# Quarter sums of the FFN's activations: formed by the producer and kept in DRAM, with the down stage's weight splits on VectorE

## The chip, the cores and the metric

The kernel runs on one core of a Trainium2 chip. The metric is the device time of one execution in microseconds (us); the time before is the median of three runs, 3012.46 us.

## What is computed

The program is a hybrid two-layer block followed by a second block. The change lies in the last stage of the second block, its feed-forward network (FFN), and in nothing else:

```python
h = rmsnorm(x, g_ffn_pre)                                   # 1024 tokens x 1024
f = (silu(h @ w_gate) * (h @ w_up)) @ w_down                # 2816 columns in between (22 rows of 128)
x = x + rmsnorm(f, g_ffn_post)
```

Below, y is the product `silu(h @ w_gate) * (h @ w_up)`, kept transposed: row j of it is a tile of 128 of the 2816 columns by 1024 tokens.

## The kernel before

**Exact products from rounded halves.** A matmul here takes operands that are split into a rounded part and a rest: `split` (line 368) lets ScalarE write the rounded copy (hi) and a second engine the difference (lo = source - hi, one subtraction with both inputs in SBUF). Each product then is three matmuls: lo by hi, hi by lo, hi by hi. Every operand of 128x512 so costs one ScalarE instruction and one subtraction, and the kernel chooses per operand which engine subtracts.

**Gate and up stage** (`ffn`, from line 2329). The 22 rows of y are made in pairs of rows. The first pair (rows 0 and 1) is made directly, over two halves of the tokens, while `combos` (line 2481) forms sums of the input's quarters on VectorE and GpSimd. The ten other pairs use a seven-product scheme: for each pair seven steps for gate (`a` = 0) and seven for up (`a` = 1), each step 12 matmuls. `pair_prep` (line 2533) prepares a step's weights two steps ahead, with their subtractions on GpSimd. VectorE adds the products' PSUM results and multiplies gate by up into the tiles `F`. When a pair is done, `store` (line 2344) sends both rows to the DRAM rows `self.F` (22 tiles of 128x1024, line 1733).

**Down stage** (`quarters`, line 1444). The product with w_down also uses seven products of quarters. The 22 rows of y are split into an upper and a lower half, and row k is taken with row 11 + k; with the two halves of the tokens this gives four quarters y11, y12, y21, y22. The seven products are done in four passes over k = 0 to 10: passes a, b and c hold two products each, pass d one. A unit is one product at one k: 12 matmuls of 128x512 in passes a to c. Pass d has 22 half units of six matmuls, the first eleven for token tiles 4 and 5, the last eleven for tiles 6 and 7, which keep the operands of the first. `quarters_units` (line 1384) prepares two units ahead:

- pass a uses y11 and y12 and plain weights;
- pass b uses the sums y21 + y22 - y11 and y11 - y21, formed in place from the rows held in SBUF (tiles `yr`), two adds on VectorE and two on GpSimd (one into `s3`), and two adds of weights on VectorE;
- pass c uses y21 + y22 and y22, and three adds of weights on VectorE;
- pass d uses y12 minus the first sum of pass b, and plain weights.

Each operand of y is split into a tile `yhl` with the subtraction on VectorE; each operand of the weights into `whi` and `wlo` (pass d: `whl`) by `w_pair` (line 1438), whose subtraction is on GpSimd. `whi` and `wlo` have three buffers each, so that the split for unit n + 3 waits until TensorE is through with unit n. All loads are issued by SyncE's queue in a fixed order. The rows of y are loaded once, in pass a (`y_row`, line 1320), and stay until pass c or d: up to 22 of the 40 tiles of 128x1024 that all stages share (`S`). Ahead of the first pass, two steps are loaded.

After pass c four token tiles (0 to 3) are complete, and `chain` (line 2454) normalizes and stores them; tiles 4 to 7 follow in pass d. A chain has ScalarE squares, a multiply by the norm's weights, a power on GpSimd and two fused adds with the residual `rx` on VectorE.

**What sets the order.** The order on TensorE is that of the program. On the other engines it comes from priorities: a planner (`Mixer`) books each instruction at a modelled time, and each queue is sorted by that. It has one table of busy times per engine, so that a change of engine moves instructions in the whole stage. Each queue then runs strictly in this order.

Of the kernel before, what the change touches and what calls it, by code (L numbers as in the profile page):

```python
# [13 lines left out]
ALU = mybir.AluOpType  # L14
AX = mybir.AxisListType

NX = 1024
# [465 lines left out]
class Layers(Base):  # L483
# [835 lines left out]

    def y_row(self, yT, order):  # L1320

        def row(k):
            r = self.S("yr")
            self.nc.sync.dma_start(out=r, in_=yT[order[k]][:, 0:NX])
            return r

        return row

    def y_prefetch(self, g, yT, order, n):
# [32 lines left out]

    def quarters_begin(self, kn, w, row):

        self.q = (kn // 2, row, {})
        self.q_ld = self.quarters_loads(w)
        self.q_ahead = deque(next(self.q_ld) for _ in range(2))

    def quarters_loads(self, w):
        m, row, rows = self.q  # L1370
        dma = self.nc.sync.dma_start
        for p in "abcd":
            for k in range(m):
                if p == "a":
                    rows[k], rows[m + k] = row(k), row(m + k)
                q = self.QW[p]
                ts = [self.S("ws") for _ in range((len(q) + 1) // 2)]
                u = [ts[i // 2][:, 512 * (i % 2):512 * (i % 2) + 512] for i in range(len(q))]
                for t, (i, j) in zip(u, q):
                    r = k + m * i  # L1380
                    dma(out=t, in_=w[j, r // 2][:, 512 * (r % 2):512 * (r % 2) + 512])
                yield ts, u

    def quarters_units(self):

        m, row, rows = self.q
        gp = self.nc.gpsimd
        sub = ALU.subtract
# [17 lines left out]
        for p in "abcd":  # L1406
            for k in range(m):
                ts, u = step()
                r1, r2 = rows[k], rows[m + k]
                y11, y21, y12, y22 = (r[:, c:c + 512] for r in (r1, r2) for c in (512, 0))  # L1410
                if p == "a":
                    yield p, 0, k, *unit(y11, u[0], [])
                    yield p, 1, k, *unit(y12, u[1], ts)
                elif p == "b":
                    tmp = self.S("s3", (128, 512))
                    self.tt(tmp, y11, y21, sub, gp)
                    self.tt(y21, y21, y22, ALU.add)
                    self.tt(y11, y21, y11, sub)
                    self.tt(y12, y12, y11, sub, gp)
                    self.tt(u[0], u[0], u[1], sub)  # L1420
                    self.tt(u[2], u[0], u[2], ALU.add)
                    yield p, 0, k, *unit(y11, u[2], [])
                    yield p, 1, k, *unit(tmp, u[0], [*ts, tmp])
                elif p == "c":
                    self.tt(u[0], u[0], u[1], sub)
                    self.tt(u[2], u[3], u[2], sub)
                    self.tt(u[2], u[2], u[0], ALU.add)
                    yield p, 0, k, *unit(y21, u[0], [])
                    yield p, 1, k, *unit(y22, u[2], [*ts, r1])
                else:  # L1430
                    t = self.S("whl", dt=F32R)
                    y, hl, old = unit(y12, u[0], [*ts, r2], (t[:, 0:512], t[:, 512:1024]))
                    keep.append((y[2:], hl, old + [t]))
                    yield p, 0, k, y[:2], hl, []
        for k, x in enumerate(keep):
# [243 lines left out]
class Block2(Layers):  # L1679
# [30 lines left out]
    def setup2(self):  # L1710
# [21 lines left out]
        self.x2 = self.dram("x2", [NX, 1024])  # L1732
        self.F = self.drams("ffn", 22, [128, NX])

# [594 lines left out]
    def ffn(self, hT):  # L2329
# [13 lines left out]

        def store(j, f):
            nc.sync.dma_start(out=self.F[j], in_=f)
            self.free(f)

        T = []
# [3 lines left out]
        for gi in range(2):  # L2352
# [7 lines left out]
            for n, (a, j) in enumerate(first):  # L2360
# [27 lines left out]
        for j, a, i in steps:  # L2388
# [7 lines left out]
            if j == 20 and a and i == self.QB:  # L2396
                self.quarters_begin(22, self.io["w_down2"], self.y_row(self.F, range(22)))
            ps = self.bank()
# [297 lines left out]
```

## Time and profile before

| | |
|---|---|
| median of 3 runs (lowest to highest) | 3012.46 us (3010.87 to 3014.09) |
| the profiled execution's own time | 3013.66 us |
| its span in the trace | 3011.9 us |
| TensorE matmuls busy | 2734.6 us (91%) |
| VectorE (DVE) busy | 1986.3 us (66%) |
| ScalarE (ACT) busy | 1185.1 us (39%) |
| GpSimd (POOL) busy | 1168.4 us (39%) |
| mean granted TensorE clock | 0.952 of full |

The trace names engines PE (TensorE matmuls), PEld (its weight loads), DVE, ACT, POOL and SPq (the DMA queue of SyncE). A row of the timeline is one instruction or a run of equal ones (xN); in brackets behind it stands how long its engine had been idle and what ended that. A name such as yhl<-yr,yhl is the output and the inputs by the program's tiles. Most lines are those of one helper (L251), so tiles tell the places apart. A matmul's duration in the trace overlaps its neighbours; how fast TensorE goes is read from the count of matmuls in a stretch.

### The profile page before, as it was taken

To read this page: it belongs to the slowest core of one execution; us is meant where nothing else is said; L and a number is where in the kernel's file an instruction comes from. 1 tells how busy PE (TensorE), PEld (TensorE's weight loads), DVE (VectorE), ACT (ScalarE), POOL (GpSimd) and SP (SyncE) were. 2 spreads that over 40 slices of the span, in tenths; PEclk is the share of its full clock that TensorE was granted. 3 is DMA by queue.
4 is the path that set the end of the run, shared out by engine and by line. 5 is a ranking of instruction groups with operands and counts; after the bars stand their busy time and mean duration, and the time that the engine had idled before them with its cause. 6 is when DMAs were issued, how large, how long until landed. Compare 5 with 4: busy or idle time off the path is not lost. (4 is left out here: it accounts for less than half of the span.)

```text
span 3011.9 us, 41163 instructions
## 1 busy us (share of the span) xinstructions
PE 2734.6 (91%) x14508; PEld 2339.8 (78%) x14508; DVE 1986.3 (66%) x3880; ACT 1185.1 (39%) x2691; POOL 1168.4 (39%) x998
## 2 busy tenths in 40 slices
PE   7989999999989989999889968898888899999888
PEld 6977888888778768887787767777767688888666
DVE  6666675684641567665555887777645777776786
ACT  5212254553442125554343323455544333334333
POOL 3345512213443451222563322111145644445755
PEclk9989999999989999999999979899999999999899
DMA  7533212225333221224444343221353222227244
GB/s 255 184 107 98 98 31 80 81 80 194 116 100 103 54 69 36 94 80 154 159 129 143 131 149 109 79 78 53 118 181 108 87 80 80 81 80 283 74 158 157
DMA packets 160975, 341.13 MB, mean 113 GB/s; under 512 B 28704, under 2 KB 56640, under 8 KB 160768
## 3 DMA queue, kind: packets, MB, share of 16 engines
q1 hardware_dynamic: 147968, 316.33, 31.1%
q10 hardware_dynamic: 10016, 13.12, 1.8%
q0 software_dynamic: 2784, 9.05, 1.0%
q8 instruction: 115, 1.88, 0.3%
q14 instruction: 92, 0.75, 0.1%
HBM read 265.46 MB, written 66.67 MB: 110 GB/s over the span
## 5 line engine op out<-in xcount | busy, mean ns | idle before, releaser
L251 POOL TENSOR_TENSOR wl<-wr,wh 128x512 fp32r<-128x512 f32 (+2 forms) x344 | 460.8, 1344 | 1142.3 <-ACT wh L251 1065.7
L344 PE MATMUL pb<-xh,wl 128*128 128x512 f32 x1456 | 579.9, 398 | 1.8 <-POOL wl L251 1.7
L344 PE MATMUL pb<-xh,wh 128*128 128x512 f32 x1456 | 578.9, 398 | 0.0
L344 PE MATMUL pb<-xl,wh 128*128 128x512 f32 x1456 | 578.4, 397 | 0.0
L251 ACT ACTIVATE wh<-wr 128x512 fp32r<-128x512 f32 (+2 forms) x344 | 203.0, 592 | 430.0 <-PE pb L344 328.2
L344 PEld LDWEIGHTS pb<-xh,wl 128*128 128x128 f32 x1456 | 277.4, 191 | 58.3 <-POOL wl L251 3.0
L344 PEld LDWEIGHTS pb<-xh,wh 128*128 128x128 f32 x1456 | 278.0, 191 | 53.4 <-issue 0.3
L344 PEld LDWEIGHTS pb<-xl,wh 128*128 128x128 f32 x1456 | 277.2, 190 | 54.0 <-issue 0.3
L344 PE MATMUL pb<-wh,yhl 128*128 128x512 f32 x832 | 266.4, 399 | 14.1 <-DVE xl L251 4.9
L344 PE MATMUL pb<-T,wh 128*128 128x512 f32 x640 | 198.1, 391 | 11.7 <-DVE T L251 10.4
L344 PEld LDWEIGHTS pb<-wh,yhl 128*128 128x128 f32 x832 | 159.7, 192 | 50.7 <-issue 8.0
L251 POOL TENSOR_TENSOR wl<-ws,wh 128x512 fp32r<-128x512 f32 x100 | 136.2, 1362 | 137.4 <-ACT wh L251 136.3
L344 PE MATMUL pb<-whi,yhl 128*128 128x512 f32 x528 | 174.5, 410 | 14.1 <-DVE yhl L251 6.1
L251 DVE TENSOR_TENSOR yhl<-yr,yhl 128x512 fp32r<-128x512 f32 (+4 forms) x122 | 116.4, 978 | 97.5 <-ACT yhl L251 93.6
L344 PE MATMUL pb<-wl,yhl 128*128 128x512 f32 x416 | 165.7, 398 | 7.3 <-POOL wl L251 7.3
L251 ACT ACTIVATE pt<-pb 128x512 fp32r<-128x512 f32 (+3 forms) x230 | 114.7, 527 | 122.9 <-PE pb L349 120.7
L251 DVE TENSOR_TENSOR pt<-pb,pt 128x512 fp32r<-128x512 f32 (+3 forms) x230 | 129.4, 596 | 49.7 <-ACT pt L251 49.0
L344 PEld LDWEIGHTS pb<-T,wh 128*128 128x128 f32 x640 | 120.5, 189 | 37.5 <-DVE T L251 10.9
L344 PEld LDWEIGHTS pb<-whi,yhl 128*128 128x128 f32 x528 | 104.9, 199 | 40.7 <-ACT whi L251 7.4
L344 PE MATMUL pb<-wl,xh 128*128 128x384 f32 (+1 forms) x384 | 127.4, 332 | 6.5 <-POOL wl L251 6.5
L251 ACT ACTIVATE wh<-ws 128x512 fp32r<-128x512 f32 x100 | 63.2, 632 | 169.8 <-PE pb L344 168.2
L344 PE MATMUL pb<-wh,xl 128*128 128x384 f32 (+1 forms) x384 | 126.4, 329 | 3.8 <-ACT wh L251 1.4
(435 smaller groups left out, 6188.7 us busy)
## 6 DMA issues: line engine op xcount, KB each, us to landing
wr<-in_w_in_dram SPq DMA_DIRECT2D x152, 256.0 KB, 2.7
ws<-in_w_down_dram SPq DMA_DIRECT2D x110, 256.0 KB, 3.8
wr<-in_w_out_dram SPq DMA_DIRECT2D x96, 256.0 KB, 2.9
wm<-in_w_modT_dram SPq DMA_DIRECT2D x32, 512.0 KB, 4.2
wr<-in_w_v_dram SPq DMA_DIRECT2D x64, 192.0 KB, 2.4
ws<-in_w_gate_dram SPq DMA_DIRECT2D x22, 512.0 KB, 5.2
ws<-in_w_up_dram SPq DMA_DIRECT2D x22, 512.0 KB, 4.8
ffn<-F SPq DMA_DIRECT2D x22, 512.0 KB, 3.0
```

What stands on the lines that cost most here:

```text
L251: return fn(*a, **kw)
L344: self.mix.product(c / 2.4, out, (lhsT, rhs), lambda: self.nc.tensor.matmul(out, lhsT, rhs, start=start, stop=stop))
```

## The change

The producer now forms the quarter sums. `pair_store` takes a finished pair of rows, forms four sums on VectorE (four adds of 128x512, with both inputs in SBUF) and stores all seven quarters side by side in one DRAM tile of 128x3584 per pair, with six stores where there were two. The two rows of a pair now are adjacent rows of y (2k and 2k + 1), and the weights are read to match. The down stage streams: each k of each pass loads its two quarters (pass d: one) into a fresh `yr`, which is freed with the step; nothing of y stays in SBUF between passes. Three steps are loaded ahead, not two. The four adds per k of pass b go. `w_pair` leaves its subtraction to VectorE: 66 `wlo` and 11 `whl` leave GpSimd. TensorE's order stays the same. The diff, cut:

```diff
-    def quarters_begin(self, kn, w, row):
-        self.q = (kn // 2, row, {})
+    def quarters_begin(self, w, y):
+        self.q = (len(y), y)
         self.q_ld = self.quarters_loads(w)
-        self.q_ahead = deque(next(self.q_ld) for _ in range(2))
+        self.q_ahead = deque(next(self.q_ld) for _ in range(3))
+    def pair_store(self, k, r1, r2):
+        sub = ALU.subtract
+        y11, y21, y12, y22 = (r[:, c:c + 512] for r in (r1, r2) for c in (512, 0))
+        a, b = self.S("ya"), self.S("yb")
+        s2, s3 = a[:, 0:512], a[:, 512:1024]
+        s1, s4 = b[:, 0:512], b[:, 512:1024]
+        self.tt(s1, y21, y22, ALU.add)
+        self.tt(s2, s1, y11, sub)
+        self.tt(s3, y11, y21, sub)
+        self.tt(s4, y12, s2, sub)
+        for c, t in ((0, y11), (512, y12), (1024, a), (2048, s1), (2560, y22), (3072, s4)):
+            self.nc.sync.dma_start(out=self.F[k][:, c:c + t.shape[1]], in_=t)
+        self.free(r1, r2, a, b)
     def quarters_loads(self, w):
...
-                if p == "a":
-                    rows[k], rows[m + k] = row(k), row(m + k)
                 q = self.QW[p]
+                yt = self.S("yr")
+                c = min(1024, 3584 - 1024 * n)
+                dma(out=yt[:, 0:c], in_=y[k][:, 1024 * n:1024 * n + c])
...
-                    r = k + m * i
-                    dma(out=t, in_=w[j, r // 2][:, 512 * (r % 2):512 * (r % 2) + 512])
+                    dma(out=t, in_=w[j, k][:, 512 * i:512 * i + 512])
...
                 elif p == "b":
-                    tmp = self.S("s3", (128, 512))
-                    self.tt(tmp, y11, y21, sub, gp)
-                    self.tt(y21, y21, y22, ALU.add)
-                    self.tt(y11, y21, y11, sub)
-                    self.tt(y12, y12, y11, sub, gp)
                     self.tt(u[0], u[0], u[1], sub)
                     self.tt(u[2], u[0], u[2], ALU.add)
...
     def w_pair(self, src, hl=None):
...
-        self.split(src, *hl, self.nc.gpsimd)
+        self.split(src, *hl)
...
-        self.F = self.drams("ffn", 22, [128, NX])
+        self.F = self.drams("ffn", 11, [128, 3584])
...
-                    if a:
-                        store(j, f[j])
+                    if a and j:
+                        self.pair_store(0, *f)
...
                 if a:
                     self.free(tu)
-                    store(j, f[0])
-                    store(j + 1, f[1])
+                    self.pair_store(j // 2, *f)
```

**VectorE while the first pair ends and `combos` finishes.** `F` are the pair's rows, `th` ScalarE's result of gate, `wt` and `ws` weights for the next steps, `bq` quarter sums of the input, `T` their rests that TensorE waits for. Before, and in the change:

```order
L251 SCALAR_TENSOR_TENSOR F_22057<-th_22352,pb_22319 128x512
L251 TENSOR_TENSOR wt_22438<-ws_22317 128x512
L251 TENSOR_TENSOR bq_22472<-xh_21526,xl_21530 128x1024
L251 TENSOR_TENSOR wt_22438<-wt_22438,ws_22315 128x512
L251 TENSOR_TENSOR bq_22476<-xh_22014,xl_22018 128x1024
L251 SCALAR_TENSOR_TENSOR F_22057<-F_22057,pb_22355 128x512
L251 TENSOR_TENSOR bq_22472<-bq_22474,bq_22472 128x1024
L251 TENSOR_TENSOR ws_22317<-ws_22315,ws_22317 128x512
```

```order
L251 SCALAR_TENSOR_TENSOR F_22046<-th_22341,pb_22308 128x512
L251 TENSOR_TENSOR wt_22426<-ws_22306 128x512
L251 TENSOR_TENSOR yb_22460<-F_22046,F_22173 128x512
L251 TENSOR_TENSOR wt_22426<-wt_22426,ws_22304 128x512
L251 TENSOR_TENSOR ws_22306<-ws_22304,ws_22306 128x512
L251 SCALAR_TENSOR_TENSOR F_22046<-F_22046,pb_22344 128x512
L251 TENSOR_TENSOR ya_22459<-yb_22460,F_22046 128x512
L251 TENSOR_TENSOR bq_22471<-xh_21515,xl_21519 128x1024
L251 TENSOR_TENSOR ya_22459<-F_22046 128x512
L251 TENSOR_TENSOR bq_22475<-xh_22003,xl_22007 128x1024
L251 TENSOR_TENSOR bq_22471<-bq_22473,bq_22471 128x1024
```

Three of the pair's four sums (`yb`, `ya`, `ya`) now stand ahead of the sums `bq` or among them; two weight subtractions of GpSimd's queue also moved ahead of its two `bq`.

**VectorE where the last pair ends and the down stage begins.** The last `th<-pb` reads the result of the last step of gate and up. Before, and in the change:

```order
L251 TENSOR_TENSOR th_25388<-pb_25371,Fu_25319 128x512
L251 TENSOR_TENSOR yhl_25474<-yr_25320,yhl_25474 128x512
L251 SCALAR_TENSOR_TENSOR F_25173<-F_25173,th_25388 128x512
L251 TENSOR_TENSOR yhl_25481<-yr_25322,yhl_25481 128x512
L251 TENSOR_TENSOR Fu_25319<-pb_25391,Fu_25319 128x512
L251 TENSOR_TENSOR yhl_25495<-yr_25327,yhl_25495 128x512
```

```order
L251 TENSOR_TENSOR th_25550<-pb_25537,Fu_25408 128x512
L251 TENSOR_TENSOR wlo_25595<-ws_25416,whi_25594 128x512
L251 SCALAR_TENSOR_TENSOR F_25262<-F_25262,th_25550 128x512
L251 TENSOR_TENSOR ya_25553<-yb_25554,F_25262 128x512
L251 TENSOR_TENSOR ya_25553<-F_25262 128x512
L251 TENSOR_TENSOR yb_25554<-F_25263,ya_25553 128x512
L251 TENSOR_TENSOR yhl_25572<-yr_25409,yhl_25572 128x512
```

Before, the first splits of y stood among the last four steps of gate and up; now the first (`yhl_25572`, for unit 0 of pass a) stands behind the last step's result and the last pair's sums. `wlo_25595` is that of unit 2.

**VectorE in pass d.** `lr<-lr,bcr` begins the chain of a token tile after pass c, the `rx` rows end it. Before (all eleven `whl` were on GpSimd, ahead of this), and in the change:

```order
L251 TENSOR_TENSOR lr_26533<-lr_26533,bcr_25465 128x512
L251 TENSOR_SCALAR rs_5703_27111<-rs_5703_27111,rs_5702_27107 128x1
L251 TENSOR_TENSOR yhl_27288<-yr_25768,yhl_27288 128x512
L251 SCALAR_TENSOR_TENSOR rx_27104<-lr_26533,rs_5704_27112,rx_27104 128x512
L251 TENSOR_SCALAR rs_5708_27129<-rs_5708_27129 128x1
L251 SCALAR_TENSOR_TENSOR rx_27104<-lr_26533,rs_5704_27112,rx_27104 128x512
L251 TENSOR_TENSOR lr_26538<-lr_26538,bcr_25465 128x512
L251 TENSOR_SCALAR rs_5709_27133<-rs_5709_27133,rs_5708_27129 128x1
L251 TENSOR_TENSOR yhl_27300<-yr_25813,yhl_27300 128x512
```

```order
L251 TENSOR_TENSOR lr_26591<-lr_26591,bcr_25565 128x512
L251 TENSOR_SCALAR rs_5720_27189<-rs_5720_27189,rs_5719_27185 128x1
L251 TENSOR_TENSOR yhl_27320<-yr_27247,yhl_27320 128x512
L251 SCALAR_TENSOR_TENSOR rx_27182<-lr_26591,rs_5721_27190,rx_27182 128x512
L251 TENSOR_SCALAR rs_5725_27207<-rs_5725_27207 128x1
L251 SCALAR_TENSOR_TENSOR rx_27182<-lr_26591,rs_5721_27190,rx_27182 128x512
L251 TENSOR_TENSOR lr_26596<-lr_26596,bcr_25565 128x512
L251 TENSOR_SCALAR rs_5726_27211<-rs_5726_27211,rs_5725_27207 128x1
L251 TENSOR_TENSOR whl_27319<-ws_27249,whl_27319 128x512
```

In the change `yhl_27320` and `whl_27319` belong to half unit 5 (counted from 0); those of half unit 6 stand in the two chains that follow, and those of 7 to 10 in one run behind the fourth chain. Before, only the y splits of half units 9 and 10 stood among the chains.

## Rows read from the trace of the kernel before

**Rows 1.** Busy us by stretch: pass a, b, c, d of the down stage.
```profile
core 0: us, PE busy (x) PEld busy (x) DVE busy (x) ACT busy (x) POOL busy (x), PEclk, DMA share, GB/s
2743.70:2803.50 59.80, 59.80 (x264) 49.27 (x263) 29.15 (x32) 25.98 (x47) 33.50 (x25) 1.00 0.65 233
2803.50:2899.00 95.50, 75.11 (x267) 56.20 (x266) 86.13 (x76) 28.13 (x54) 75.33 (x47) 0.87 0.31 102
2899.00:2970.50 71.50, 63.61 (x265) 50.56 (x265) 55.27 (x64) 31.92 (x56) 41.24 (x29) 0.95 0.54 176
2970.50:3000.10 29.60, 29.60 (x132) 24.53 (x131) 24.22 (x42) 8.67 (x24) 13.39 (x13) 1.00 0.46 172
```
**Rows 2.** Waits of PE, then of DVE, passes b and c: total us, times, longest.
```profile
PE pb L344 <- POOL wlo L251: 14.2, 12, 3.0
PE pb L344 <- DVE yhl L251: 6.1, 2, 4.2
...
DVE ws L251 <- DMA ws<-in_w_down_dram: 9.6, 7, 2.7
```
**Rows 3.** Timeline of DVE and POOL in pass b: start, us, engine, instruction.
```profile
2830.48 1.62 POOL L251 TENSOR_TENSOR s<-yr 128x512 f32<-128x512 f32 x1
2830.88 1.77 DVE L251 TENSOR_TENSOR ws<-ws,ws 128x512 f32<-128x512 f32 x1
2832.06 1.73 POOL L251 TENSOR_TENSOR wlo<-ws,whi 128x512 fp32r<-128x512 f32 x1
2832.57 1.77 DVE L251 TENSOR_TENSOR yr<-yr,yr 128x512 f32<-128x512 f32 x1
...
2834.38 0.69 DVE L251 TENSOR_TENSOR yr<-yr 128x512 f32<-128x512 f32 x1
2834.99 0.69 DVE L251 TENSOR_TENSOR ws<-ws 128x512 f32<-128x512 f32 x1
```
**Rows 4.** Timeline of DVE where one pair of rows ends, gate and up stage.
```profile
2401.18 0.69 DVE L251 TENSOR_TENSOR th<-pb,Fu 128x512 f32<-128x512 f32 x1 [0.35 <-PE pb L344]
...
2403.48 0.68 DVE L251 TENSOR_TENSOR ws<-ws,wt 128x512 f32<-128x512 f32 x1
2406.69 0.69 DVE L251 TENSOR_TENSOR F<-pb,F 128x512 f32<-128x512 f32 x1 [2.53 <-PE pb L344]
```
**Rows 5.** Busy us in 25 us of the same stage.
```profile
2400.00:2425.00 25.00, 25.00 (x112) 20.68 (x111) 17.45 (x21) 9.19 (x15) 12.17 (x10) 1.00 0.34 126
```
**Rows 6.** Timeline of DVE and PE where the sums of the input finish.
```profile
2346.47 0.67 DVE L251 SCALAR_TENSOR_TENSOR F<-th,pb 128x512 f32<-128x512 f32 x1
...
2362.59 5.71 DVE L251 TENSOR_TENSOR T<-bq,T 128x1024 fp32r<-128x1024 f32 x2 [0.84 <-ACT T L251]
...
2365.05 1.22 PE L344 MATMUL pb<-T,wh 128*128 128x512 f32 x2 [10.43 <-DVE T L251]
```
**Rows 7.** Timeline of PE and ACT at the start of the down stage.
```profile
2743.47 0.39 PE L344 MATMUL pb<-xh,wl 128*128 128x512 f32 x1
2743.70 0.39 PE L344 MATMUL pb<-whi,yhl 128*128 128x512 f32 x1
...
2743.72 0.63 ACT L251 ACTIVATE whi<-ws 128x512 fp32r<-128x512 f32 x1 [1.04 <-POOL wlo L251]
```
**Rows 8.** Busy us in 10 us of pass b, around TensorE's longest wait for y.
```profile
2820.00:2830.00 10.00, 6.48 (x16) 5.08 (x17) 9.91 (x12) 3.90 (x7) 7.53 (x5) 0.66 0.23 79
```
**Rows 9.** Timeline of DVE and PE in pass d.
```profile
2968.27 6.66 DVE L251 TENSOR_TENSOR lr<-pb,lr 128x512 f32<-128x512 f32 x11
...
2970.50 30.08 PE L344 MATMUL pb<-whl,yhl 128*128 128x512 f32 x132
...
2976.69 0.68 DVE L251 TENSOR_TENSOR yhl<-yr,yhl 128x512 fp32r<-128x512 f32 x1
...
2980.95 0.68 DVE L251 TENSOR_TENSOR yhl<-yr,yhl 128x512 fp32r<-128x512 f32 x1
```
**Rows 10.** Busy us in 10 us of pass a; last number GB/s moved.
```profile
2760.00:2770.00 10.00, 10.00 (x46) 8.26 (x45) 3.00 (x5) 4.51 (x8) 4.74 (x4) 1.00 1.03 401
```

More of the change, by code (lines that the diff above doesn't have):

```diff
@@ L1318, in y_load @@
         return r
[L1320 to L1327, printed above, removed]
     def y_prefetch(self, g, yT, order, n):
@@ L1361 @@
     QW = {"a": ((0, 0), (1, 0)), "b": ((1, 1), (0, 1), (0, 0)), "c": ((0, 1), (0, 0), (1, 1), (1, 0)), "d": ((1, 1),)}
-    def quarters_begin(self, kn, w, row):
-        self.q = (kn // 2, row, {})
+    def quarters_begin(self, w, y):
+        self.q = (len(y), y)
         self.q_ld = self.quarters_loads(w)
-        self.q_ahead = deque(next(self.q_ld) for _ in range(2))
+        self.q_ahead = deque(next(self.q_ld) for _ in range(3))
[12 more added lines that the diff above has]
+        self.free(r1, r2, a, b)
     def quarters_loads(self, w):
-        m, row, rows = self.q
+        m, y = self.q
         dma = self.nc.sync.dma_start
-        for p in "abcd":
+        for n, p in enumerate("abcd"):
             for k in range(m):
-                if p == "a":
-                    rows[k], rows[m + k] = row(k), row(m + k)
                 q = self.QW[p]
+                yt = self.S("yr")
+                c = min(1024, 3584 - 1024 * n)
+                dma(out=yt[:, 0:c], in_=y[k][:, 1024 * n:1024 * n + c])
                 ts = [self.S("ws") for _ in range((len(q) + 1) // 2)]
@@ L1379, in quarters_loads @@
                 for t, (i, j) in zip(u, q):
-                    r = k + m * i
-                    dma(out=t, in_=w[j, r // 2][:, 512 * (r % 2):512 * (r % 2) + 512])
-                yield ts, u
+                    dma(out=t, in_=w[j, k][:, 512 * i:512 * i + 512])
+                yield [yt, *ts], yt, u
     def quarters_units(self):
-        m, row, rows = self.q
-        gp = self.nc.gpsimd
+        m = self.q[0]
         sub = ALU.subtract
@@ L1407, in quarters_units @@
             for k in range(m):
-                ts, u = step()
-                r1, r2 = rows[k], rows[m + k]
-                y11, y21, y12, y22 = (r[:, c:c + 512] for r in (r1, r2) for c in (512, 0))
+                ts, yt, u = step()
+                y1, y2 = yt[:, 0:512], yt[:, 512:1024]
                 if p == "a":
-                    yield p, 0, k, *unit(y11, u[0], [])
-                    yield p, 1, k, *unit(y12, u[1], ts)
+                    w1, w2 = u
                 elif p == "b":
-                    tmp = self.S("s3", (128, 512))
-                    self.tt(tmp, y11, y21, sub, gp)
-                    self.tt(y21, y21, y22, ALU.add)
-                    self.tt(y11, y21, y11, sub)
-                    self.tt(y12, y12, y11, sub, gp)
                     self.tt(u[0], u[0], u[1], sub)
                     self.tt(u[2], u[0], u[2], ALU.add)
-                    yield p, 0, k, *unit(y11, u[2], [])
-                    yield p, 1, k, *unit(tmp, u[0], [*ts, tmp])
+                    w1, w2 = u[2], u[0]
                 elif p == "c":
@@ L1427, in quarters_units @@
                     self.tt(u[2], u[2], u[0], ALU.add)
-                    yield p, 0, k, *unit(y21, u[0], [])
-                    yield p, 1, k, *unit(y22, u[2], [*ts, r1])
+                    w1, w2 = u[0], u[2]
                 else:
                     t = self.S("whl", dt=F32R)
-                    y, hl, old = unit(y12, u[0], [*ts, r2], (t[:, 0:512], t[:, 512:1024]))
+                    y, hl, old = unit(y1, u[0], ts, (t[:, 0:512], t[:, 512:1024]))
                     keep.append((y[2:], hl, old + [t]))
                     yield p, 0, k, y[:2], hl, []
+                    continue
+                yield p, 0, k, *unit(y1, w1, [])
+                yield p, 1, k, *unit(y2, w2, ts)
         for k, x in enumerate(keep):
@@ L2342, in up @@
             self.stt(d, d, 0.5, u, ALU.mult, ALU.mult)
-        def store(j, f):
-            nc.sync.dma_start(out=self.F[j], in_=f)
-            self.free(f)
         T = []
@@ L2396, in ffn @@
             if j == 20 and a and i == self.QB:
-                self.quarters_begin(22, self.io["w_down2"], self.y_row(self.F, range(22)))
+                self.quarters_begin(self.io["w_down2"], self.F)
             ps = self.bank()
```

## The prediction

> **What bounds the kernel now.** I read the busy times by stretch first, because the change touches one stage. In pass a TensorE is busy throughout and does 264 matmuls in 59.8 us [rows 1], which is 0.2265 us each, 2.72 us a unit of 12. Passes b and c hold as many each and take 95.5 and 71.5 us. So the two passes lose 95.5 + 71.5 - 2 x 59.8 = 47.4 us against pass a. Pass d runs at full pace again: 132 matmuls in 29.6 us, 1.345 us a half unit.
>
> Then the waits: in passes b and c TensorE waits mostly for GpSimd's `wlo`, then for VectorE's `yhl` [rows 2]. The waits are only part of the 47.4 us; the rest is the clock, granted at 0.87 and 0.95 there [rows 1]. Ten us around the longest wait show its price: 16 matmuls took 6.48 busy us [rows 8], where 16 x 0.2265 = 3.62 would do, so TensorE ran at its lower level, 1.2 GHz, after it had stood still, and a wait of 4 us costs up to 2.86 us more.
>
> Then why two engines that have time to spare on the average are late. VectorE is busy 86.1 of 95.5 us in pass b [rows 1]. The timeline shows what fills it: while GpSimd works on the same sort of operands, one VectorE instruction starts each 2832.57 - 2830.88 = 1.69 us and GpSimd takes 1.62 to 1.73; with GpSimd idle the next VectorE instruction starts after 2834.99 - 2834.38 = 0.61 us [rows 3]. The two take turns. Pass b needs 8 VectorE and 4 GpSimd instructions per k, and 8 at 0.61 would be 4.9 us of the 5.44 us that TensorE needs; taking turns makes it 95.5 / 11 = 8.7.
>
> **The change, part by part.** *Passes b and c.* GpSimd loses all its `wlo`, its two adds per k in pass b, and all `whl`. Left for it there are four multiplies of `lr`. VectorE loses two adds per k in pass b and takes over two `wlo`: with the splits of y (2) and the weight adds (2 and 3) it has 6 per k in pass b and 7 in pass c. At 0.61 us that is 3.7 and 4.3 us per k, under 5.44. TensorE then sets the pace, as in pass a: -47.4 us. I give 4 us back for the joints between the passes, where VectorE also empties eight banks (4.9 us), and for loads that come late. The bounds are 0 and 9.6 us, the time for which VectorE waited for weights before [rows 2]; I take a little under the middle, since the tiles that held y are now free for loads.
>
> *Pairs in the gate and up stage.* Ten of the eleven pairs add four adds and four DMA issues inside a stretch in which TensorE never pauses [rows 5]. VectorE is busy 17.5 of 25 us there, and at a pair's end it is idle 2.53 us [rows 4], room for three adds of 0.61 to 0.8 us; one that meets GpSimd costs 1.69. What is late next is the emptying of one of eight PSUM banks and weights that are wanted two steps on. I cost this at nothing; if that cover is gone, it is the third rival. The stores stand ahead of the next pair's weight loads on SyncE's queue and hold them back by a few us, and those weights are wanted a whole pair later: nothing.
>
> *The first pair.* Here VectorE is the bound: from 2346.47 to the rest `T` at 2362.59 it hardly stops, and TensorE waits 10.43 us for that [rows 6]. Three adds now stand among its work: 1.8 us at 0.61, 5.1 us at 1.69. The two subtractions that moved ahead on GpSimd delay one of its sums, too. I take 3 us, bounds 0 and 6.
>
> *The start of the down stage.* Before, TensorE went on without a gap, 2743.47 to 2743.70 [rows 7]. Now seven VectorE instructions stand between the end of the last step and the first rest of y: `th`, `wlo`, `F`, `ya`, `ya`, `yb`, `yhl`. GpSimd has nothing left, so 7 x 0.61 = 4.3, with the last one's tail 4.4 us; `wlo` waits for a ScalarE `whi` that comes 0.6 us after the same step [rows 7], which fits behind `th`. A wait of that length also costs the clock's 2.86 us [rows 8]. Sum 7.3 us, bounds 3 and 9.
>
> *Pass d.* VectorE began to empty the banks 2.2 us before pass d and came to the first split of y among the chains 2976.69 - 2970.50 = 6.2 us after its start; the next stood one chain later, 4.26 us [rows 9]. The changed order holds one split per chain at the same places, but they belong to half units 5 and 6. The second operand of 5 starts at 6.2 + 4.26 = 10.5 and is there at 11.1, when TensorE has been ready since 5 x 1.345 = 6.7. That of 6 starts at 6.2 + 3 x 4.26 = 19.0. The chain ends at 23.2; eight more splits at 0.61 end at 28.1, and the last half unit at 29.5, where 11 x 1.345 = 14.8 would do. Loss 14.7 us. The second eleven half units reuse what is there. The bounds: 8 us if chains without other GpSimd work run faster, 22 with two clock penalties of 2.86 us and a late load.
>
> *Transfers.* Stores and loads of y grow by 3584 to 2048 columns. Passes b and c now need 1.31 and 1.57 MB per k (512 KB of y, three or four times 256 KB of weights), together 31.7 MB in 119.6 us, 265 GB/s. Ten us of pass a moved 401 GB/s while TensorE ran at full pace [rows 10]. Cost nothing, second rival otherwise.
>
> The sum: -47.4 + 4 + 3 + 7.3 + 14.7 = -18.4 us. Against the profiled execution's 3013.66 us this is 2995.3; the median of the runs lies 1.2 us below that execution, so the forecast is **2994 us**.
>
> **The rivals.** *First, VectorE becomes the bound.* All 143 adds and splits of passes b and c are on one engine now. The costs above, 25 us (3 + 7.3 + 14.7), are paid in any case; the gain covers them as long as the two passes take under 167 - 25 = 142 us, or one VectorE instruction per 0.99 us. At the pace of rows 3 with both engines at work, 1.69 us, they would take 242 us: +74.6 + 25 = +100 us, 3112 us. For it: VectorE is already the busiest engine beside TensorE in pass b. Against it: the pace of 0.61 comes exactly where GpSimd is idle [rows 3]. Chance 0.05, slower. The Trainium skill (Perfetto Trace Analysis, Optimizing Scalar/DVE Operations) says that with a saturated VectorE moving some work to ScalarE or even GpSimd may make sense, which speaks against this change; the same paragraph warns that between VectorE and GpSimd it might not help, as they share a read port. By its advice the time would be this rival's; the trace bears out the warning.
>
> *Second, loads become the bound.* VectorE's queue takes weight adds of later steps in a fixed order, so a late load also stops the splits behind it. It decides below 31.7 MB / 142 us = 223 GB/s. At the mean of pass c, 176 GB/s [rows 1], the passes would take 180 us: +13 + 25 = +38, 3050 us. Against it stand the 401 GB/s [rows 10]; for it that VectorE did wait 9.6 us for weights at a lower rate [rows 2]. Chance 0.09, slower.
>
> *Third, the gate and up stage pays.* If each of nine pairs loses what three adds at 1.69 exceed the idle 2.53 us by, that is 9 x 2.5 = 23 us: 3017 us, about as before. Against it: eight banks. Chance 0.06.
>
> *Fourth, the new waits don't bite.* If the first splits and those of pass d come early enough, only 4 and 3 us are given back: 3012.5 - 40.4 = 2972 us. The queue's order speaks against it. Chance 0.14.
>
> *Fifth, the change doesn't do what it says*: b and c are held by something else, such as ScalarE's order, and the time stays. ScalarE is busy 28 of 95.5 us [rows 1]. Chance 0.04.
>
> **How the numbers follow.** The forecast has 0.62. Its own bounds, with 0 to 9.6, 0 to 6, 3 to 9 and 8 to 22, run from -36 to -1 us, 2976 to 3012. The fourth rival adds the lower end. The range of 2970 to 3010 leaves out the first three rivals and the worst corner, under 0.2. A measurement of this kernel can tell 0.2%, 6 us, from no change. Faster: the forecast but for its upper corner, and the fourth, 0.62 - 0.02 + 0.14, and 0.07 for milder forms of the second and third, 0.81. Within 0.2%: 0.02 of the forecast, the fifth and part of the third, 0.08. Slower: 0.11.
>
> **What would show it.** Right: in the stretch of passes b and c about 528 matmuls in some 124 us with the clock near 1; VectorE's `wlo` and `yhl` near 0.68 us each; a wait of TensorE for `yhl` of 4 to 5 us at the start of the down stage; waits for `whl` in the first half of pass d, which takes 40 to 46 us in all; the wait for `T` at 13 us instead of 10.4. Wrong: `wlo` on VectorE over 1 us; VectorE waiting for loads of `ws` or `yr` for more than 10 us; gaps of TensorE in the gate and up stage; a pass d of 30 us.

## The result, and the profile after

The changed kernel takes 2991.2 us, the median of four runs (2989.88 to 2993.76), beside 3013.28 us before, which is now the median of four runs as well (3010.87 to 3018.62): a ratio of 0.9921, 95% interval 0.9909 to 0.9933, or 20 to 27 us less by the ratio. The forecast was 2994 us.

The profiled execution took 2993.76 us. Read the stretches of the down stage first, as in [rows 1]: passes a, b, c and d of the changed kernel.

```profile
core 0: us, PE busy (x) PEld busy (x) DVE busy (x) ACT busy (x) POOL busy (x), PEclk, DMA share, GB/s
2757.52:2818.95 61.43, 61.43 (x265) 50.79 (x266) 34.06 (x54) 26.62 (x47) 0.00 (x0) 0.98 0.90 332
2818.95:2878.75 59.80, 59.80 (x266) 49.51 (x265) 52.20 (x83) 27.25 (x52) 5.60 (x4) 1.00 0.78 259
2878.75:2938.55 59.80, 59.80 (x266) 49.51 (x265) 50.13 (x82) 30.39 (x54) 0.00 (x0) 1.00 0.68 223
2938.55:2980.70 42.15, 34.23 (x133) 26.14 (x131) 28.37 (x48) 11.24 (x28) 10.12 (x10) 0.88 0.35 125
```

Passes b and c, 95.5 and 71.5 us in [rows 1], now take 59.8 each: TensorE never pauses and holds its full clock. Pass d went the other way, from 29.6 to 42.15 us. TensorE's waits from 2330 us, in the FFN, to the end (who is waited for; total us, times, longest):

```profile
PE pb L344 <- DVE T L251: 16.1, 1, 16.1
PE pb L344 <- DVE yhl L251: 7.4, 2, 4.5
PE pb L344 <- DVE whl L251: 4.9, 2, 3.5
```

The 14.2 us for GpSimd's `wlo` of [rows 2] are gone. In their place stand waits for VectorE at the start of the down stage and in pass d. VectorE by kind of instruction in passes b and c (count | busy us, mean ns of one | idle before it, and for what):

```profile
L251 DVE TENSOR_TENSOR yhl<-yr,yhl 128x512 fp32r<-128x512 f32 x47 | 32.8, 731 | 0.0
L251 DVE TENSOR_TENSOR wlo<-ws,whi 128x512 fp32r<-128x512 f32 x42 | 29.9, 712 | 16.6 <-ACT whi L251 16.6
L251 DVE TENSOR_TENSOR ws<-ws 128x512 f32<-128x512 f32 x29 | 19.4, 684 | 0.0
```

A subtraction takes 0.71 to 0.73 us here, where [rows 3] show VectorE instructions of 1.77 us beside a working GpSimd. VectorE waits for no load; its only larger wait is for ScalarE's `whi`, which each `wlo` needs.

**How the runs are compared below.** Before the FFN the instructions of the changed kernel stand in the same order on every engine as before. Yet its first FFN matmuls (the transposes that wait 1.96 us for `rr`) come at 2320.45 us, against 2314.51 before, and over all the profiles of this study they lie between 2305.84 and 2320.70. That scatter is as large as most terms here, so the parts are read from the FFN alone. Each column is a difference of start times in the trace: from those matmuls to the first matmul with the last `T`; from there to the first unit of pass a; passes a to c; pass d and the tail to the end of the span; and the sum. All in us.

| kernel | to T | gate and up | a to c | d and tail | FFN |
|---|---|---|---|---|---|
| before | 50.54 | 378.65 | 226.80 | 41.40 | 697.39 |
| changed | 53.56 | 383.51 | 181.03 | 53.45 | 671.55 |
| splits only | 50.55 | 378.68 | 200.76 | 50.44 | 680.43 |
| sums only | 53.59 | 383.90 | 184.92 | 53.36 | 675.77 |
| first units early | 53.61 | 379.24 | 183.53 | 52.99 | 669.37 |
| chains late | 53.58 | 383.49 | 181.03 | 42.20 | 660.30 |
| first pair late | 50.56 | 383.19 | 182.50 | 52.61 | 668.86 |
| idle adds | 53.61 | 383.37 | 209.52 | 53.12 | 699.62 |
| idle writes, 2 per k | 53.57 | 383.43 | 181.05 | 53.83 | 671.88 |
| idle writes, 6 per k | 53.60 | 384.00 | 181.28 | 39.58 | 658.46 |
| idle multiplies | 53.56 | 383.41 | 185.73 | 53.15 | 675.85 |
| order mended | 50.51 | 378.57 | 179.52 | 42.23 | 650.83 |
| mended, splits on GpSimd | 50.54 | 379.16 | 181.03 | 45.12 | 655.85 |
| before, 3 ahead | 50.54 | 379.22 | 230.23 | 45.60 | 705.59 |

At TensorE's full pace passes a to c are 3 x 59.8 = 179.4 us. In the changed kernel the FFN is 25.84 us shorter.

The start of the down stage in the changed kernel: the timeline of VectorE, from the last step's result `th` on, and TensorE's first unit.

```profile
2753.04 0.69 DVE L251 TENSOR_TENSOR th<-pb,Fu 128x512 f32<-128x512 f32 x1
2753.65 0.68 DVE L251 TENSOR_TENSOR wlo<-ws,whi 128x512 fp32r<-128x512 f32 x1
2754.24 0.68 DVE L251 SCALAR_TENSOR_TENSOR F<-F,th 128x512 f32<-128x512 f32 x1
2754.96 0.69 DVE L251 TENSOR_TENSOR ya<-yb,F 128x512 f32<-128x512 f32 x1
2755.57 0.68 DVE L251 TENSOR_TENSOR ya<-F 128x512 f32<-128x512 f32 x1
2756.17 0.68 DVE L251 TENSOR_TENSOR yb<-F,ya 128x512 f32<-128x512 f32 x1
2756.78 1.89 DVE L251 TENSOR_TENSOR yhl<-yr,yhl 128x512 fp32r<-128x512 f32 x3
2757.52 0.79 PE L344 MATMUL pb<-whi,yhl 128*128 128x512 f32 x1 [4.52 <-DVE yhl L251]
```

These are the seven instructions of the prediction in their order, one each 0.6 us. Behind the wait TensorE ran at its lower level, 1.2 GHz: the granted clock of the next 3 us (7 matmuls where 13 would fit) is 0.50.

```profile
2757.50:2760.50 3.00, 2.98 (x7) 2.40 (x8) 1.77 (x3) 0.00 (x0) 0.00 (x0) 0.50 0.84 246
```

And pass d, first TensorE, then the four splits on VectorE for half units 5 and 6; for the last three of them it waited:

```profile
2938.55 7.19 PE L344 MATMUL pb<-whl,yhl 128*128 128x512 f32 x31
2947.19 1.43 PE L344 MATMUL pb<-whl,yhl 128*128 128x512 f32 x5 [1.45 <-DVE whl L251]
2951.55 0.66 PE L344 MATMUL pb<-whl,yhl 128*128 128x512 f32 x1 [2.93 <-DVE yhl L251]
2955.70 25.02 PE L344 MATMUL pb<-whl,yhl 128*128 128x512 f32 x95 [3.49 <-DVE whl L251]
```

```profile
2942.19 0.68 DVE L251 TENSOR_TENSOR yhl<-yr,yhl 128x512 fp32r<-128x512 f32 x1
...
2946.46 0.68 DVE L251 TENSOR_TENSOR whl<-ws,whl 128x512 fp32r<-128x512 f32 x1
...
2950.73 0.68 DVE L251 TENSOR_TENSOR yhl<-yr,yhl 128x512 fp32r<-128x512 f32 x1
...
2954.97 0.67 DVE L251 TENSOR_TENSOR whl<-ws,whl 128x512 fp32r<-128x512 f32 x1
```

There is one split per chain, 4.24 to 4.27 us apart, while each half unit of 1.345 us wants two of them.

### The profile page after: what moved, and what is told of

It reads as the page before. It is cut to its first block, busy times and chain, and to the rows that moved or that the text cites. A ratio compares the mean times of both kernels' runs of the same rounds, so it can differ in the third digit from the quotient of the medians.

```text
span 2992.0 us, 41172 instructions
## 1 busy us (share of the span) xinstructions
PE 2729.9 (91%) x14508; PEld 2342.2 (78%) x14508; DVE 1987.7 (66%) x3979; ACT 1185.6 (40%) x2691; POOL 1023.4 (34%) x899
## 5 line engine op out<-in xcount | busy, mean ns | idle before, releaser
L344 PE MATMUL pb<-T,wh 128*128 128x512 f32 x640 | 198.1, 391 | 16.1 <-DVE T L251 16.1
L344 PE MATMUL pb<-whi,yhl 128*128 128x512 f32 x528 | 163.8, 391 | 4.5 <-DVE yhl L251 4.5
L251 DVE TENSOR_TENSOR yhl<-yr,yhl 128x512 fp32r<-128x512 f32 (+2 forms) x133 | 98.1, 765 | 63.6 <-ACT yhl L251 63.3
L344 PE MATMUL pb<-wh,xh 128*128 128x384 f32 (+1 forms) x384 | 125.4, 327 | 0.0
```

Of the source, the lines that this page charges most:

```text
L251: return fn(*a, **kw)
L344: self.mix.product(c / 2.4, out, (lhsT, rhs), lambda: self.nc.tensor.matmul(out, lhsT, rhs, start=start, stop=stop))
```

## The experiments

**Splits only.** The kernel before, with the weight subtractions on VectorE:

```diff
-        self.split(src, *hl, self.nc.gpsimd)
+        self.split(src, *hl)
```

> One part alone: the kernel before, with only the subtractions of the down stage's weights moved from GpSimd to VectorE. Rows of y stay in SBUF and their sums are formed in place, two adds on VectorE and two on GpSimd per k of pass b. Theory (the two engines take turns while both work on SBUF operands, 1.69 us per VectorE instruction, 0.61 us alone): pass c has no GpSimd work left and goes at TensorE's pace, 59.8 us instead of 71.5; pass b has 8 VectorE instructions per k of which 2 meet GpSimd, 2 x 1.69 + 6 x 0.61 = 7.0 us per k, 77 us instead of 95.5; pass d loses 5 to 8 us, because the last splits for half unit 10 stand behind the fourth chain; nothing is lost in the gate and up stage and under 2 us at the start of the down stage. Sum -30 + 7 + 1 = -22 us, 2991 us. Rival (it is the rows formed ahead and streamed that win, not the engine of the splits): pass c stays at 71.5 us and the time within 6 us of 3013.

Measured: 0.9921 of the kernel before (0.9898 to 0.9943); the FFN is 17.0 us shorter. Passes b and c:

```profile
2802.50:2883.66 81.16, 66.79 (x267) 50.62 (x267) 76.37 (x99) 27.28 (x53) 39.09 (x23) 0.96 0.32 108
2883.66:2943.46 59.80, 59.80 (x264) 49.12 (x263) 57.00 (x95) 34.92 (x61) 0.00 (x0) 1.00 0.67 224
```

With no GpSimd work left, pass c goes at TensorE's pace, though the rows of y stay in SBUF here as before; pass b, which keeps two GpSimd adds per k, takes 81 us (77 expected). The rival falls. Pass d and the tail pay 9.0 us (5 to 8 expected).

**Sums only.** The changed kernel, with the weight subtractions back on GpSimd:

```diff
-        self.split(src, *hl)
+        self.split(src, *hl, self.nc.gpsimd)
```

> The other part alone: the changed kernel, with the subtractions of the down stage's weights back on GpSimd. Theory: passes b and c keep two GpSimd subtractions per k that meet VectorE, so wlo stays at about 1.6 us and pass c at about 71 us; pass b has 4 VectorE and 2 GpSimd instructions per k instead of 6 and 4 and comes to 62 to 71 us; the first pair costs 3 us, the start of the down stage 4 to 6, pass d 6 to 8 (six splits of y among or behind the chains). Sum -25 to -36 from the two passes, +15 given back: 2992 to 3003 us, likeliest 2999. Rival (the sums formed ahead and the streaming are the whole gain): passes b and c take 119.6 us together, and with less VectorE work in pass d the time is 2985 us or less.

Measured: 0.9926 (0.9910 to 0.9942), the FFN 21.6 us shorter. The median, 2997 us, lies in the expected range, but by luck, since both theories missed. Passes a to c take 184.92 us, only 3.9 more than in the changed kernel, so pass c did not stay at 71; but pass d and the tail take as long as in the changed kernel, 53.36 us or 12.0 more than before where 6 to 8 were expected, with no `whl` on VectorE. The engines still take turns, as the rows of VectorE and GpSimd in the timeline of pass b show:

```profile
2848.93 1.78 POOL L251 TENSOR_TENSOR wlo<-ws,whi 128x512 fp32r<-128x512 f32 x1 [1.12 <-ACT whi L251]
2849.49 1.77 DVE L251 TENSOR_TENSOR ws<-ws 128x512 f32<-128x512 f32 x1
2851.36 0.69 DVE L251 TENSOR_TENSOR ws<-ws,ws 128x512 f32<-128x512 f32 x1
2851.64 1.56 POOL L251 TENSOR_TENSOR wlo<-ws,whi 128x512 fp32r<-128x512 f32 x1 [0.92 <-ACT whi L251]
```

VectorE still takes 1.77 us beside a `wlo`. But with four or five VectorE and two GpSimd instructions per k (2 x 1.69 + 3 x 0.61 = 5.2 us) this fits into TensorE's 5.44. So either part of the change alone gives back more than half of the 47.4 us, and the two gains do not add up: 26.0 us in passes a to c by the splits, 41.9 by the sums, 45.8 by both.

**First units early.** The last two steps of gate and up prepare no further pair; the first two units of pass a go there:

```diff
...
-            w += [x for x in [next(prep, None)] if x]
+            x = next(prep, None)
+            if x:
+                w.append(x)
+            else:
+                if units is None:
+                    units = self.quarters_units()
+                self.q_first.append(next(units))
...
-        units = self.quarters_units()
-        q = deque(next(units) for _ in range(2))
+        q = self.q_first
...
```

> The changed kernel with the first two units of pass a prepared during the last two steps of gate and up (in the two places where no further pair is prepared), so that the first two splits of y stand ahead of the last pair's sums on VectorE. Theory: the wait of 4.5 us for yhl goes, and with it the 1.6 us at the lower clock behind it: 6.1 us less, 2985 us. Rival (the wait moves to the next operand, wlo or the second yhl behind the same sums): 2 to 4 us of waiting stay at the second or third unit, 2988 to 2991 us.

Measured: 0.9894 (0.9876 to 0.9911), the FFN 2.2 us shorter than the changed kernel's. The rival was right: the first unit starts without a gap (gate and up 379.24 us), and the wait moved to the third, whose split stands behind the same sums.

```profile
2757.49 1.89 DVE L251 TENSOR_TENSOR yhl<-yr,yhl 128x512 fp32r<-128x512 f32 x3
2758.23 0.50 PE L344 MATMUL pb<-whi,yhl 128*128 128x512 f32 x1 [2.05 <-DVE yhl L251]
```

**Chains late.** The chains of token tiles 0 to 3 get a lower priority and nothing else changes:

```diff
-                        self.mix.add(chain(t), True, peak=1)
+                        self.mix.add(chain(t), True, peak=1, late=20000.0 if p == "c" else 0.0)
```

> The changed kernel with the chains of token tiles 0 to 3 given a priority 20 us later, so that all splits of pass d stand ahead of them on VectorE; no work is added or taken away. Theory (pass d pays for the order of the queue, not for the amount of VectorE work): 12 splits at 0.61 us end 10 us after the pass began, before half unit 10 wants them at 13.5, so pass d takes 29.6 to 31 us instead of 42.2; the chains behind it add 0 to 2 us at the end: 2978 to 2982 us. Rival (VectorE has more work than pass d has time): pass d shortens, but the chains run out behind it, and the end moves by less than 4 us: 2987 to 2991 us.

Measured: 0.9869 (0.9854 to 0.9884), 2979.13 us; pass d:

```profile
2938.80:2968.45 29.65, 29.65 (x132) 24.57 (x131) 26.63 (x47) 11.47 (x28) 9.51 (x10) 1.00 0.42 147
```

All of it came back, with the same work on VectorE: pass d and the tail 42.20 instead of 53.45 us. Pass d pays for the queue's order, not for its amount of work.

**First pair late.** The first pair's sums and stores are issued three steps into gate and up:

```diff
-                    if a and j:
-                        self.pair_store(0, *f)
+        first_f = f
...
+            if (j, a, i) == (2, 0, 3):
+                self.pair_store(0, *first_f)
```

> The changed kernel with the sums and stores of the first pair issued three steps into the gate and up stage, so that they stand behind the sums of the input on VectorE. Theory (three adds among VectorE's work delay the last T): TensorE starts the first step with T 50.5 us after the FFN's first matmuls, as in the kernel before, not 53.6; 3.0 us less, 2988 us. Rival (GpSimd's subtractions, which moved ahead of its own sums, set that wait, not the three adds): under 1 us less. If the four adds now hold up the emptying of banks in the first steps, a new gap shows there and the time is that of the changed kernel.

Measured: 0.9899 (0.9881 to 0.9916). The time to T is 50.56 us, that of the kernel before, and TensorE waits 10.46 us there: the 3.0 us are those of the adds. The sums cost nothing where they now stand (gate and up 383.19 us). The FFN is 2.7 us shorter and not 3.0, because passes a to c took 182.50 us against 181.03: behind the same wait of 4.52 us at the start of the down stage the granted clock was 0.50 for the second 3 us as well, where the changed kernel had 1.00.

```profile
2742.59:2745.59 3.00, 3.00 (x8) 2.33 (x8) 0.00 (x0) 0.47 (x1) 0.00 (x0) 0.50 1.03 393
```

**Idle adds.** Two GpSimd adds per k of passes b and c, whose result no engine uses:

```diff
+                if p in "bc":
+                    dm = self.S("dm")
+                    for h in range(2):
+                        self.tt(dm[:, 512 * h:512 * h + 512], y1, y2, ALU.add, self.nc.gpsimd)
+                    self.free(dm)
```

> The changed kernel with two more adds per k on GpSimd in passes b and c (both quarters of y from SBUF into a scratch tile) for whose result nobody waits; as many instructions as the subtractions that the change took away from GpSimd. Theory (taking turns): each of them holds a VectorE instruction up, so per k of pass b 2 x 1.69 + 4 x 0.61 = 5.8 us and of pass c 2 x 1.69 + 5 x 0.61 = 6.4 us, over the 5.44 that TensorE needs: passes b and c 64 and 71 us, +10 to +16, some 3003 to 3008 us, and VectorE's yhl and wlo at over 1 us in the mean. Rival (GpSimd's work costs only where its result is waited for): passes b and c stay at 119.6 us, 2991 us.

Measured: 1.0014 (1.0004 to 1.0024): the whole gain is gone. In pass b, the timeline of VectorE, then of GpSimd:

```profile
2827.40 1.63 DVE L251 TENSOR_TENSOR ws<-ws 128x512 f32<-128x512 f32 x1
2829.07 1.65 DVE L251 TENSOR_TENSOR ws<-ws,ws 128x512 f32<-128x512 f32 x1
2830.64 1.78 DVE L251 TENSOR_TENSOR wlo<-ws,whi 128x512 fp32r<-128x512 f32 x1
2832.34 1.77 DVE L251 TENSOR_TENSOR yhl<-yr,yhl 128x512 fp32r<-128x512 f32 x1
```

```profile
2820.04 13.52 POOL L251 TENSOR_TENSOR dm<-yr 128x512 f32<-128x512 f32 x8
```

GpSimd works through eight adds at 1.69 us each, and VectorE keeps step with it. Passes b and c, and the commonest VectorE instruction in them:

```profile
2810.60:2958.68 148.08, 128.72 (x530) 101.21 (x528) 142.90 (x164) 57.64 (x105) 78.32 (x46) 0.97 0.59 198
```

```profile
L251 DVE TENSOR_TENSOR yhl<-yr,yhl 128x512 fp32r<-128x512 f32 x47 | 46.9, 1030 | 0.0
```

VectorE is busy 142.9 us, 40.6 more than the 52.20 + 50.13 of the changed kernel, for 42 adds: 0.97 us each in the mean. Its idle time is 4.5 us for ScalarE's `whi` and none for a load. The passes grew by 28.5 us where 10 to 16 were expected; that sum had left out the 19 PSUM evacuations and five `whl` (11.7 and 3.4 us by the same view).

**Idle writes.** The control: memsets of the quarters once they are split. The edit, cut:

```diff
...
+                if p in "bc":
+                    for y in (y1, y2):
+                        self.nc.gpsimd.memset(y, 0.0)
...
```

> Control to the run with idle adds: two memsets per k on GpSimd in passes b and c, into the quarters of y once they are split, which read nothing. If what the engines share is the reading of SBUF, VectorE's yhl and wlo stay at 0.68 to 0.8 us and passes b and c at 119.6 us; if any GpSimd instruction makes VectorE wait, it looks like the run with idle adds.

Measured, in one execution, as in the next two runs: passes a to c take 181.05 us, and VectorE's `yhl` 731 ns in the mean. The memsets cost nothing. As two of them keep GpSimd busy for 1.05 us per k only, the next run had six:

```diff
-                    for y in (y1, y2):
+                    for y in (y1, y2) * 3:
```

> Control of equal weight to the run with idle adds: six memsets per k on GpSimd in passes b and c, which keep it busy for some 6 x 0.53 = 3.2 us per k, nearly as long as two adds (2 x 1.74 = 3.5), and read nothing. Theory (the reading of SBUF is what the two engines take turns at): VectorE's yhl and wlo stay at 0.7 to 0.8 us in the mean and passes b and c at 119.6 us. Rival (GpSimd being busy is enough): VectorE near 1 us, passes b and c over 130 us.

Measured, in passes b and c:

```profile
L251 POOL MEMSET yr<- 128x512 f32 x129 | 63.8, 527 | 55.5 <-DVE yhl L251 49.8 <-issue 3.4
```

```profile
L251 DVE TENSOR_TENSOR yhl<-yr,yhl 128x512 fp32r<-128x512 f32 x48 | 33.5, 730 | 0.0
```

GpSimd is busy 63.8 us with them, nearly as long as with the adds (72.0 us), and VectorE does not notice. So a busy GpSimd is not enough: what holds VectorE up here is instructions that read SBUF. This run also showed pass d a second time: VectorE's queue now has all splits of pass d ahead of the chains' multiplies and adds, and pass d with the tail takes 39.58 us. That the planner moved them because it books the memsets on GpSimd, where each chain has its multiply, is likely but was not shown.

**Idle multiplies.** The idle adds, with one input instead of two:

```diff
-                        self.tt(dm[:, 512 * h:512 * h + 512], y1, y2, ALU.add, self.nc.gpsimd)
+                        self.ts(dm[:, 512 * h:512 * h + 512], (y1, y2)[h], 1.0, None, ALU.mult, eng=self.nc.gpsimd)
```

> The run with idle adds once more, with two multiplies by a constant per k on GpSimd in place of the two adds, so that each reads one SBUF operand, not two. Theory (any reading of SBUF by GpSimd takes its turn with VectorE's two-input instructions): VectorE's mean is over 0.85 us and passes b and c are lengthened by more than 5 us. Rival (only GpSimd's instructions with two inputs take turns): as with memsets, 119.6 us and 0.73 us.

Measured: between the two. Passes a to c are 4.7 us longer, and VectorE's `yhl` takes 828 ns in the mean. Beside a run of multiplies (1.64 us each) the timeline has:

```profile
2837.96 0.68 DVE L251 TENSOR_TENSOR ws<-ws 128x512 f32<-128x512 f32 x1
2838.68 0.98 DVE L251 TENSOR_TENSOR ws<-ws,ws 128x512 f32<-128x512 f32 x1
2839.58 1.70 DVE L251 TENSOR_TENSOR yhl<-yr,yhl 128x512 fp32r<-128x512 f32 x2
```

Some instructions are held up by 0.3 to 0.4 us and some not at all. VectorE is busy 116.20 us, 13.9 more for 42 multiplies: 0.33 us each in the mean, a third of what an add with two inputs costs. By its signs the theory fell short (0.828 us where it had over 0.85, 4.7 us where it had over 5), and the rival, no cost at all, did not come either.

**Order mended.** First units early, first pair late, chains late, and the last pair's sums at k = 2 of pass a:

```diff
-                    self.pair_store(j // 2, *f)
+                    if j < 20:
+                        self.pair_store(j // 2, *f)
...
+            if (p, i, k) == ("a", 0, 2):
+                self.pair_store(m - 1, *f)
```

> The changed kernel with its three costs taken away by order alone: the first pair's sums behind the sums of the input, the first two units of pass a prepared in the last two steps of gate and up and the last pair's sums behind unit 2 of pass a, the chains of token tiles 0 to 3 behind the splits of pass d. Theory (the three costs are independent): 3.0 + 6.5 + 11.3 = 20.8 us less than the changed kernel, 2970 us, 0.9855 of the kernel before. Rival (a mended wait shows up one stage on, as the wait for y did at the start of the down stage): two of the three remain in part, 2975 to 2982 us.

Measured: 2968.2 us, 0.9849 of the kernel before (0.9826 to 0.9872), and the FFN is 20.7 us shorter than the changed kernel's (20.8 expected). The four passes:

```profile
2744.77:2804.57 59.80, 59.80 (x266) 49.53 (x265) 34.98 (x56) 25.58 (x45) 0.00 (x0) 1.00 0.79 280
2804.57:2864.37 59.80, 59.80 (x266) 49.52 (x265) 52.20 (x83) 27.25 (x52) 5.64 (x4) 1.00 0.80 259
2864.37:2924.17 59.80, 59.80 (x265) 49.53 (x264) 50.14 (x82) 30.39 (x54) 0.00 (x0) 1.00 0.69 223
2924.17:2953.80 29.63, 29.63 (x132) 24.57 (x131) 26.62 (x47) 11.46 (x28) 9.45 (x10) 1.00 0.40 147
```

TensorE does not pause from the first matmul with the last `T` to the last half unit. This version is faster than both kernels.

**The same, splits on GpSimd.** The order mended, with the one edit of the run with sums only:

```diff
-        self.split(src, *hl)
+        self.split(src, *hl, self.nc.gpsimd)
```

> The version with the three costs mended by order, with the subtractions of the down stage's weights back on GpSimd. Theory (with the sums formed ahead, 4 or 5 VectorE and 2 GpSimd instructions per k fit into TensorE's 5.44 us even when they take turns: 2 x 1.69 + 3 x 0.61 = 5.2): passes b and c take 0 to 5 us more than with all splits on VectorE, pass d no more; 2968 to 2974 us, 0.985 to 0.987 of the kernel before. Rival (the move of the splits is worth its own part of the gain): passes b and c take over 8 us more, 2976 us or above.

Measured: 0.9865 (0.9843 to 0.9886), which the runs alone cannot tell from the version above. The FFN is 5.0 us longer: 0.6 in gate and up, 1.5 in passes a to c, as the theory has it, but 2.9 in pass d and the tail, where it had none: the last evacuation starts at 2961.95 us, 2.6 after TensorE has ended, since VectorE is still at the late chains.

**Before, three steps ahead.** The kernel before, in `quarters_begin`:

```diff
-        self.q_ahead = deque(next(self.q_ld) for _ in range(2))
+        self.q_ahead = deque(next(self.q_ld) for _ in range(3))
```

> The kernel before, with three steps loaded ahead of pass a instead of two, as in the change. Theory (the loads of passes b and c are late because tiles come free late, not because they are asked for late): within 5 us of the kernel before, passes b and c at 160 to 170 us. Rival (the depth of loading ahead is a part of the gain): VectorE's 9.6 us of waiting for weights goes, passes b and c 6 to 15 us shorter.

Measured: 1.0020 (1.0006 to 1.0034). Passes a to c take 230.23 us, 3.4 more, and VectorE waits 11.9 us for weights (9.6 in [rows 2]). The FFN is 8.2 us longer, a little past the 5 us expected, and the rival falls. Deeper loading by itself gains nothing; the changed kernel with only two steps ahead was not run.

## Why the prediction was right, step by step

**What bounds the kernel.** For pass b, where 35.7 of the 47.4 us were lost, the reading of [rows 1 to 3] held: it was slow because VectorE and GpSimd took turns, and the idle adds show what that costs without any wait for a result. The Trainium skill (SBUF — State Buffer, Who interferes with whom) says that a VectorE instruction with two SBUF inputs contends with a GpSimd instruction that reads SBUF, not with one that only writes it. The adds and the memsets agree: 0.97 us for each add, nothing for 129 memsets. One number in that part was wrong: I gave pass b eight VectorE instructions per k. Of the 76 of [rows 1] four are evacuations of PSUM and four are small ones of a chain; the other 68 make six per k. It changed no term, since the six and seven of the changed kernel were counted rightly.

For pass c of the kernel before, the reading was too simple. Its 11.7 us were not lost evenly, as with engines that take turns at every k, but mostly in one place:

```profile
2899.00:2929.00 30.00, 30.00 (x131) 24.53 (x132) 28.26 (x33) 11.12 (x19) 12.87 (x9) 1.00 0.53 175
2929.00:2941.00 12.00, 6.79 (x20) 4.78 (x19) 10.08 (x14) 5.21 (x10) 4.46 (x4) 0.72 0.54 178
2933.83 0.80 PE L344 MATMUL pb<-whi,yhl 128*128 128x512 f32 x1 [4.41 <-ACT whi L251]
2933.91 2.69 POOL L251 TENSOR_TENSOR wlo<-ws,whi 128x512 fp32r<-128x512 f32 x2 [9.79 <-ACT whi L251]
```

TensorE goes at full pace for 30 us, then stands still for 4.41 us, waiting for a `whi` of ScalarE, and goes on at a lower clock; GpSimd had been idle for 9.79 us by then. The 20 matmuls of these 12 us would fit into 4.5, so some 7.5 us are lost here. VectorE, slowed by the turns, was busy 28.26 of the first 30 us, so they may have had a part in this stop; that is not shown.

**Passes b and c**, -47.4 us, with 4 given back for joints and late loads. The gain came in full, 2 x 59.8 us, and nothing was given back. The 4 us are a term that was mis-sized: VectorE's 9.6 us of waiting for weights in [rows 2] went with the rest, as the bound of 0 had allowed.

**Pairs in the gate and up stage**, nothing. Without the 4.52 us wait at its end the stage takes 378.99 us, before 378.65. Right, and with it the third rival is out.

**The first pair**, 3 us: 53.56 - 50.54 = 3.02. The wait for `T` grew by more, from 10.43 to 16.1 us, since the two short waits of 1.26 and 0.87 us ahead of it went. What TensorE loses is read from the times of its matmuls, not from one wait.

**The start of the down stage**, 7.3 us: 4.86 in the gate and up column and 181.03 - 179.4 = 1.63 at the lower clock, 6.5 in all. The clock's price was 1.6 us here, where I took 2.86 from [rows 8]; with the first pair late it was 182.50 - 179.4 = 3.1 us behind the same wait, so no single figure would have fitted.

**Pass d**, 14.7 us: 42.15 - 29.60 = 12.55, less 0.5 from a shorter tail. The mechanism was right: one split per chain, 4.26 us apart in the mean, as forecast. But the first came 3.6 us after the pass began, where I had 6.2: VectorE emptied eight banks in a row ahead of the first chain, not the eleven of [rows 9]. And the cause was put too narrowly: the run with sums only pays the same without `whl` on VectorE, and the one with splits only pays 9.0 without streaming y. Each part alone leaves splits among the chains for which TensorE waits.

**Transfers**, nothing: 259 and 223 GB/s flowed in passes b and c and VectorE waited for no load.

Sum: -47.4 + 3.0 + 6.5 + 12.5 - 0.5 = -25.9 us in the FFN against the -18.4 of the prediction; 4 of the 7.5 us are the joints, 2.7 pass d with the tail, 0.8 the start of the down stage. The medians differ by 22.1 us, within the 20 to 27 of the interval. That the total came within 3 us of the forecast, closer than its parts, is partly luck: the time before the FFN scatters by more than the difference.

**The rivals.** The first (VectorE the bound) did not come: its instructions took 0.73 us in the mean, and it decided at 0.99. With the idle adds the two passes took 148 us, over the 142 from which that rival decides, and the kernel was 1.0014 of the one before. The fourth had 2972 us if no new wait bites; it did not come by itself, but with the three orders mended the time was 2968.2. The Trainium skill (Perfetto Trace Analysis, Optimizing Scalar/DVE Operations) says that offloading work from a saturated VectorE to GpSimd may make sense, and that between those two it might not help. Here the warning held: the splits alone, moved the other way, made the FFN 17.0 us shorter.

What stays open: why TensorE stopped in pass c of the kernel before, with no more VectorE and GpSimd instructions per k than the run with sums only, which did the pass at nearly full pace. Deeper loading does not help. The tiles that the rows of y hold are not enough by themselves, since the run with splits only holds them too and takes 59.8 us; whether they matter together with GpSimd's splits, or whether it is the backlog of pass b, was not tried.

## What to carry to other kernels

Count what two engines do to each other, not only what each has to do: in this kernel, taking an instruction with two SBUF inputs off GpSimd gave VectorE back some 1 us (0.97 by the idle adds), more than the 0.7 us that the instruction cost it. When work moves to the engine that also runs the consumers' queue, look at each joint between stages for the first operand that now stands behind work with no deadline; here three such places cost 22 us, and a change of order alone, with the same work, gave 20.7 back. Compare single profiles stage by stage from a common event: the time before the FFN scattered by 15 us with the same instructions in the same order.

## What was not expected of the hardware

A GpSimd multiply with one SBUF input holds VectorE's two-input instructions up too, but by 0.33 us each in the mean against 0.97 for an add with two inputs, though both keep GpSimd busy for about 1.7 us (1680 and 1739 ns in the mean). And TensorE's return to full clock behind a wait of 4.5 us cost 1.6 us in the changed kernel, where the granted clock was 0.50 for the first 3 us and 1.00 in the next, but 3.1 us behind an equal wait of 4.52 us in the run with the first pair late, where it was 0.50 for 6 us. [rows 8] gave 2.86 us for a wait of 4.2 us. The length of the wait alone does not set the price.
